# A normalisation cut into steps of one feature tile, which a written order calls between the products at every stage boundary; squares and modulation are deferred

## The chip, the cores and the metric

The kernel runs on one core of one Trainium2 chip. The metric is the device time of one launch in microseconds (us); a number given for a kernel is the median of its runs.

## The reference, cut to what matters

Two layers of a diffusion backbone. Context tokens (128) and latent tokens (512) go through the same weights, with a modulation row of their own each.

```python
mod = einsum('bd,de->be', silu(cond), w_mod) + b_mod
sh1, sc1, g1, sh2, sc2, g2 = split(mod, 6)
h = rms_norm(x, norm1) * (1 + sc1) + sh1
# three branches from h @ w_in: Fourier mixing, gated linear attention, differential attention
merged = gf * y_f + gg * y_g + gd * y_d
x = x + g1 * (merged @ w_out)
h2 = rms_norm(x, norm2) * (1 + sc2) + sh2
ff = (silu(h2 @ w_ff_gate) * (h2 @ w_ff_up)) @ w_ff_down
x = x + g2 * ff
```

`rms_norm` divides a token by the root of the mean of its 1024 squared features. So a layer has two points at which every feature of a token must be there before the next product can start: between `w_out` and the FFN, and between the FFN and the mixer of the next layer. The second layer has no mixer behind it.

## The kernel before, in words

**Tiles.** Activations lie with features on the partitions: 8 tiles (`KT`) of 128 features by 640 tokens. Tokens are worked in two halves of 320, `SPLIT[0]` and `SPLIT[1]`, called p=0 and p=1; p=0 holds the 128 context tokens and 192 latent ones, which have different modulation, so that its instructions often come as a piece of 128 and a piece of 192. Every f32 operand is split into a high part (a cast to a reduced format, on ACT: `wh`, `ah`, `mh`, `h2h`) and a low part (the rest, a subtraction: `wl`, `al`, `ml`, `h2l`), and a product is three matmuls, high-high, high-low and low-high (`acc3`, L471; `advance_to`, L495, for one k step of a product). A product of 320 tokens over 8 feature tiles is 24 matmuls. Weights are loaded by SP into `raw`, cast by ACT (L429) and subtracted by POOL (L433); `used(l, u)` gives a weight's buffers free and starts the split of the weight that is due next. Some FFN weights need sums of blocks first, which DVE makes (L401, L402).

**Order.** PE's order is the order of the code in the whole kernel. In the FFN, DVE, ACT and POOL take their work in the order of the code too (`FFN_ORDERED`); elsewhere a scheduler orders those three. Each engine works in its order, so that an instruction that waits holds up everything behind it on its engine.

**Side work.** `queue(gen)` sets a generator on a side list, of which `slot(cols)` runs one step after each 250 columns of products. `back` is a background generator that `slot` steps after each `rate` columns; `fill` is one that the FFN steps after each group of a down projection that `groups % 4` lets through.

**Stages of a layer.** The mixer ends with the merges (`merge`, L1369 and L1370, on gates `tg`, sums `mg`, products `y`), and w_out follows: 16 products in `NORM_ORDER`, four tiles with both halves, then tiles 4 to 7 of p=0, then those of p=1. After each, `residual` (L1392, DVE) adds it to x, ACT stores x, ACT squares it (L757) and DVE adds the square to `acc` (L758). After the last product of a half, the normalisation `modulate` is queued. Its first step, `norm_diag`, sums `acc` over the partitions with three small matmuls (L766), scales the sums (`ms_v`, L768), takes the reciprocal root in ten small DVE steps (`rs_y`, L613 to L617) and spreads it on a diagonal (`diag`, L771). The second step, `norm_rows`, makes of the diagonal a row for all partitions (L784) and runs through all eight feature tiles: in front of the FFN with `norm_keep` (DVE L797, ACT L799 and L800, low part on DVE or POOL L802), in front of the mixer with `norm_apply` (DVE L847, low part L855 to L859).

**FFN.** `ffn_start` (L1511) makes 4 units of p=0 together, k step by k step, in four half banks of the two `big` PSUM tiles, then 3 units of p=1 in two `main` banks and one `misc` bank. Units are gate and up in turn; `evict` takes them out of PSUM with tanh on ACT, gate (L1559) and up (L1561) on DVE, and a split (L464 ACT, L465 DVE) into the activations `ah`, `al`; `tt` is the tile that they work on. Between them `combine` makes sums of h2 for later Strassen products (`gated`, with its sums `e`, L558). An FFN has four parts, each closed by a down projection into residuals (L1392) and, in the last part, by the squares and the normalisation of the next mixer (`done`).

**Modulation.** `mod_next` makes modulation rows: for each of the 128-feature tiles 16 to 47, per layer, two loads `rawm` and four DVE products (`junk`, L734, 128x512) whose accumulators are added to a mod row (L738). For layer 1, tiles 16 to 39 are made as `fill` in the FFN of layer 0, and tiles 40 to 47 as background work at the start of the mixer of layer 1, at a rate of one step each 320 columns. The first mixer products (`units`, `advance`) use the same four half banks.

## Time and profile before

| | before |
|---|---|
| median of 3 runs | 2406.77 us (2403.03 to 2408.39) |
| the profiled execution | 2402.18 us, of it 2400.4 in the span of the engines |
| PE (matmul), PEld (weight load) | 2244.5 us (94%), 2194.4 us (91%) |
| DVE | 1636.1 us (68%) |
| ACT | 999.8 us (42%) |
| POOL | 964.0 us (40%) |
| DMA | mean 113 GB/s |
| mean granted clock of PE | 0.974 |

The busy time of an engine is the sum of its instructions; the share is that of the span. A granted clock of 1.00 is 2.4 GHz, 0.50 is 1.2 GHz. Layer 0 reaches from 0 to about 1200 us, its FFN from about 740; the FFN of layer 1 begins at about 1940.

### The profile page before, as it was taken

What the parts mean: (1) busy time and instruction counts of PE and PEld (TensorE: products, weight loads), DVE (VectorE), ACT (ScalarE), POOL (GpSimd) and SP (SyncE); (2) the same over time, 40 slices, a digit from 0 to 9 for tenths busy, and PEclk for the clock granted to TensorE, in tenths of its full rate; (3) what the DMA queues carried; (4) which work ended last, traced back from release to release, by engine and by line L of the source; (5) the groups of instructions that cost most, each with busy time, mean ns of one, the idle gap of its engine ahead of it and who ended that gap; (6) DMA issues with size and microseconds to landing.
All of it is one profiled execution on the core that took longest, in us unless ns stands there. A gap on an engine that the chain in (4) does not pass through costs nothing.

```text
span 2400.4 us, 44466 instructions
## 1 busy us (share of the span) xinstructions
PE 2244.5 (94%) x16882; PEld 2194.4 (91%) x16882; DVE 1636.1 (68%) x3398; ACT 999.8 (42%) x2194; POOL 964.0 (40%) x783
## 2 busy tenths in 40 slices
PE   6988999999998899999969999999999988999999
PEld 4888899999997889999968999999999978999999
DVE  5896887676945768778678766876742457475674
ACT  3443546454334424242424545464543344242432
POOL 1344644353324423442433445443523235352533
PEclk9999999999998999999979999999999989999999
DMA  7442221213522272836334322212113221524433
GB/s 266 154 144 85 81 72 54 67 54 104 191 90 86 69 252 84 271 112 211 127 117 141 109 75 72 69 54 67 54 62 115 88 85 56 173 85 162 136 106 123
DMA packets 151381, 271.39 MB, mean 113 GB/s; under 512 B 19200, under 2 KB 31360, under 8 KB 151168
## 3 DMA queue, kind: packets, MB, share of 16 engines
q1 hardware_dynamic: 125824, 219.75, 28.4%
q10 hardware_dynamic: 25344, 48.80, 5.8%
q8 instruction: 133, 2.18, 0.4%
q14 instruction: 80, 0.66, 0.1%
HBM read 235.98 MB, written 27.79 MB: 110 GB/s over the span
## 4 chain that ended last, share of the span: by engine, by line
PE 63%; DVE 18%; issue 6%; ACT 4%; POOL 4%; DMA 3%; ACTq 0%; SPq 0%; POOLq 0%; DVEq 0%
PE main L471 45%; PE misc L471 8%; DVE junk L734 4%; PE big L1279 2%; PE misc L1330 2%; POOL wl L433 1%; DMA x<-xd 1%; POOL ek L1066 1%; DVE w L1211 1%; ACT wh L429 1%; PE big L987 1%; DVE x L1392 1%; DVE tg L1369 1%; PE misc L1310 1%; PE big L495 1%
## 5 line engine op out<-in xcount | busy, mean ns | idle before, releaser
L433 POOL TENSOR_TENSOR wl<-raw,wh 128x512 fp32r<-128x512 f32 x514 | 710.3, 1395 | 1072.9 <-ACT wh L429 857.9
L429 ACT CAST wh<-raw 128x512 fp32r<-128x512 f32 x518 | 316.8, 619 | 275.1 <-PE main L471 187.2
L471 PE MATMUL main<-hh,wh 128*128 128x320 f32 x960 | 302.5, 315 | 2.2 <-DVE aT L1449 2.2
L471 PE MATMUL main<-hh,wl 128*128 128x320 f32 x960 | 297.4, 310 | 0.0
L471 PE MATMUL main<-hl,wh 128*128 128x320 f32 x960 | 297.3, 310 | 0.0
L471 PE MATMUL main<-wh,hh 128*128 128x256 f32 x800 | 234.7, 293 | 7.6 <-ACT tm L604 4.7
L471 PE MATMUL main<-ah,wh 128*128 128x320 f32 x704 | 223.5, 317 | 18.5 <-DVE x L1392 18.4
L471 PE MATMUL main<-wl,hh 128*128 128x256 f32 x800 | 229.1, 286 | 0.0
L471 PE MATMUL main<-wh,hl 128*128 128x256 f32 x800 | 228.9, 286 | 0.0
L734 DVE SCALAR_TENSOR_TENSOR junk<-rawm,cond 128x512 bf16<-128x512 f32 x256 | 217.1, 848 | 14.5 <-DMA rawm<-in_w_modt_dram 10.0
L471 PE MATMUL main<-al,wh 128*128 128x320 f32 x704 | 220.7, 314 | 0.0
L471 PE MATMUL main<-ah,wl 128*128 128x320 f32 x704 | 220.6, 313 | 0.0
L1392 DVE SCALAR_TENSOR_TENSOR x<-main,g,x 128x128 f32<-128x128 f32 (+2 forms) x240 | 96.8, 435 | 163.9 <-PE main L471 151.2
L429 ACT CAST wh<-big 128x512 fp32r<-128x512 f32 x152 | 89.2, 587 | 254.0 <-DVE big L412 75.0
L471 PE MATMUL main<-h2h,wh 128*128 128x320 f32 x536 | 171.0, 319 | 18.1 <-DVE tt L1559 17.6
L471 PEld LDWEIGHTS main<-hh,wh 128*128 128x128 f32 x960 | 181.2, 189 | 2.9 <-DVE aT L1449 2.6
L471 PEld LDWEIGHTS main<-hl,wh 128*128 128x128 f32 x960 | 181.1, 189 | 0.1
L471 PEld LDWEIGHTS main<-hh,wl 128*128 128x128 f32 x960 | 180.8, 188 | 0.0
L471 PE MATMUL main<-h2l,wh 128*128 128x320 f32 x536 | 169.6, 316 | 0.0
L471 PE MATMUL main<-h2h,wl 128*128 128x320 f32 x536 | 169.4, 316 | 0.0
L471 PEld LDWEIGHTS main<-wh,hh 128*128 128x128 f32 x800 | 156.1, 195 | 10.4 <-ACT tm L604 5.3
L471 PEld LDWEIGHTS main<-ah,wh 128*128 128x128 f32 x704 | 135.1, 192 | 23.7 <-DVE x L1392 11.7
(340 smaller groups left out, 6127.1 us busy)
## 6 DMA issues: line engine op xcount, KB each, us to landing
raw<-in_w_dram SPq DMA_DIRECT2D x556, 256.0 KB, 2.9
rawm<-in_w_modt_dram SPq DMA_DIRECT2D x128, 256.0 KB, 4.5
x<-xd ACTq DMA_DIRECT2D x64, 320.0 KB, 4.5
rawm<-in_w_mod_dram SPq DMA_DIRECT2D x64, 256.0 KB, 5.4
xd<-x ACTq DMA_DIRECT2D x48, 320.0 KB, 4.1
xd<-x ACTq DMA_DIRECT2D x48, 160.0 KB, 2.0
cond<-in_cond_b_dram SPq DMA_DIRECT2D x16, 256.0 KB, 4.8
x<-in_x_t_dram SPq DMA_DIRECT2D x12, 320.0 KB, 5.7
```

Source lines behind the costliest of these rows:

```text
L429: nc.scalar.copy(h, raw)
L433: (nc.vector if late or sums else nc.gpsimd).tensor_sub(lo, raw, h.bitcast(F32))
L471: mm = lambda w, x, first=False, last=False: nc.tensor.matmul(ps, w, x, start=first and not more, stop=last, skip_group_check=more)
L495: self.nc.tensor.matmul(ps, a, b, start=(k == 0 and n == 0), stop=(k == KT - 1 and n == 2))
L734: nc.vector.scalar_tensor_tensor(self.sm([P, 512], "junk", 1, mybir.dt.bfloat16), raw, 1.0, cond[i, k], op0=ALU.mult, op1=ALU.mult, accum_ ...
L987: nc.tensor.matmul(ps[64 * x : 64 * x + 64, o : o + 64], kk[r, ks], qq[r, qs], start=True, stop=True)
L1066: nc.gpsimd.tensor_mul(ek, ek, k)
L1211: nc.vector.tensor_mul(hv(wm)[:, :, a, b], hv(x[:, 1:])[:, :, a, 1 - b], hv(sn)[:, :, a, b])
L1279: nc.tensor.matmul(S[:, x], q[:, c : c + P], k, start=(y == 0), stop=(y == 1))
L1310: nc.tensor.transpose(ps[:, o + (x - a) * P : o + (x - a + 1) * P], p[:, x * P : (x + 1) * P], self.c("ident"))
L1330: nc.tensor.matmul(ps, wT[:, x * P : (x + 1) * P], v, start=(x == 0), stop=(x == n - 1))
L1392: nc.vector.scalar_tensor_tensor(x[:, r], ps[:, r.start - s.start : r.stop - s.start], g[:, m, i : i + 1], x[:, r], op0=ALU.mult, op1=ALU.add)
```

## The change

The normalisation becomes a generator that stops behind the diagonal (it yields -3), and then behind each feature tile (`norm_keep` and `norm_apply` yield the index of the last tile whose low part is made). `upto(norm, k)` runs it to tile k in the order of the code on DVE, ACT and POOL. At w_out the steps of p=0 are called between the products of p=1: the diagonal behind product (4,1), then up to tile 0, 2 and 4 behind (5,1), (6,1) and (7,1). In the last down projection of the FFN they are called up to the diagonal, not at all, and up to tile 0 and 1. `first_four` then makes the first four units of the FFN, and of the mixer of layer 1, with the rest of the tiles a k step ahead of their use; the diagonal of p=1 is made behind k=1, its rows and tiles from k=4 on. The square of a tile is taken one product later, and its add two products later. `Gated` takes the first units of the FFN out in another order: gate, gate, up, up, then the low parts, which POOL makes; the eighth product (unit 3 of p=1) goes into a half bank of a `big` tile. The modulation of layer 1 is `fill` for tiles 16 to 31 only, in other groups and not in the last part, and tiles 32 to 47 are made in the mixer of layer 1 from the last gates on, one step each 256 columns.

```diff
+class Gated:
+    def __init__(self, kernel):
+        self.nc, self.tt, self.out = kernel.nc, kernel.unit("tt"), kernel.pairs("a", 1)[0]
+    def gate(self, ps, p):
+        t = self.tt[:, SPLIT[p]]
+        self.nc.scalar.activation(t, ps, AF.Tanh, scale=0.5)
+        self.nc.vector.scalar_tensor_tensor(t, t, 1.0, ps, op0=ALU.add, op1=ALU.mult)
+    def up(self, ps, p):
+        s = SPLIT[p]
+        self.nc.vector.tensor_mul(self.tt[:, s], self.tt[:, s], ps)
+        self.nc.scalar.copy(self.out[0][:, s], self.tt[:, s])
+    def low(self, p):
+        s = SPLIT[p]
+        self.nc.gpsimd.tensor_sub(self.out[1][:, s], self.tt[:, s], self.out[0][:, s].bitcast(F32))
...
+    def first_four(self, l, us, act, norms):
+        self.begin(l, us)
+        first, self.banks = self.banks, None
+        for k in range(KT):
+            self.upto(norms[0], min(k + 1, KT - 1))
+            for i in range(4):
+                self.advance_to(first[i], act, k, i)
+            if k == 1:
+                self.upto(norms[1], -3)
+            elif k >= 4:
+                self.upto(norms[1], k - 5)
+            if k % 2:
+                self.slot(HT)
+        second = [b[:, :HT] for b in (self.main(), self.main(), self.misc())]
+        for k in range(KT):
+            self.upto(norms[1], min(k + 1, KT - 1))
+            for i in range(3):
+                self.advance_to(second[i], act, k, i, 1)
+            if k % 2:
+                self.slot(HT)
+        return first, second
...
+    def squares(self, acc, x, s, m):
+        sq, add = self.square_add(acc, x, s, m == 0)
+        self.after(1, sq)
+        self.after(2, add)
+        if m == KT - 1:
+            self.behind(True)
...
+            yield x - 1
...
     def modulate(self, xs, acc, scale, mod, shift0, p, out, keep=False):
 
-        yield
         dg = self.norm_diag(acc, STARTS[p])
-        yield
+        yield -3
         rb = self.norm_rows(self.misc(), dg[:, : 2 * P], dg[:, 5 * 64 : 6 * 64])
-        with self.tc.manual_schedule(engines={mybir.EngineType.DVE, mybir.EngineType.Activation}):
-            if keep:
-                self.norm_keep(xs, rb, scale, mod, shift0, p, out)
-            else:
-                self.norm_apply(xs, rb, scale, mod, shift0, p, out, range(KT), lambda k: k % 4 == 1)
+        if keep:
+            yield from self.norm_keep(xs, rb, scale, mod, shift0, p, out)
+        else:
+            yield from self.norm_apply(xs, rb, scale, mod, shift0, p, out, range(KT), lambda k: k % 4 == 1)
+    def upto(self, norm, k):
+        with self.tc.manual_schedule(engines=FFN_ORDERED):
+            while norm[1] < k:
+                norm[1] = next(norm[0])
...
-        if len(backs) > 1:
-            self.finish_back()
-            self.back, self.rate = backs[1], 128
+        self.finish_back()
+        self.back, self.rate = backs[1], 128 if l == 0 else 256
...
+        first, second = self.first_four(l, us[:4], h2, norms)
+        acts = [pair(f) for f in range(AHEAD // 2)]
+        for f in range(2):
+            acts[f].gate(first[2 * f], 0)
+        for f in range(2):
+            acts[f].up(first[2 * f + 1], 0)
+        next(combine)
+        for f in range(2):
+            acts[f].low(0)
+        self.used(l, us[0])
+        self.used(l, us[1])
+        acts[0].gate(second[0], 1)
+        acts[1].gate(second[2], 1)
+        acts[0].up(second[1], 1)
+        last = self.big()[:, :HT]
+        self.group_to(last, self.weight(l, us[3]), h2, SPLIT[1])
+        next(combine)
+        acts[0].low(1)
+        acts[1].up(last, 1)
+        self.used(l, us[2])
...
-                if last:
-                    done(xs, m, s)
-                elif p == 0:
+                if not last and p == 0:
                     nc.scalar.dma_start(self.xd[m * P : (m + 1) * P], xs.pop(m))
                     load(m + 2)
                 half.add(m)
-                if fill is not None and groups % 4:
+                if last:
+                    self.behind()
+                    done(xs, m, s)
+                elif fill is not None and groups % 5:
...
+            mg, x2 = self.mixer(l, h, small, (None, later_mod(32, 48)) if l else (later_mod(16, 36), later_mod(36, 48)), norms)
...
+            def norm_steps(m, p, gen, *at):
                 if m == KT - 1:
-                    self.queue(self.modulate(x2, acc, scale2, mod, 24, p, h2, True))
-                self.slot(s.stop - s.start)
+                    norms.append([gen(p), -4])
+                if m > 3 and p and at[m - 4] is not None:
+                    self.upto(norms[0], at[m - 4])
+            with self.tc.manual_schedule(engines=FFN_ORDERED):
+                for m, p in NORM_ORDER:
+                    s = SPLIT[p]
+                    self.residual(x2[m], self.group(self.weight(l, U_OUT + m), 0, KT, mg, s), s, g1, m)
+                    self.behind()
+                    nc.scalar.dma_start(self.xd[m * P : (m + 1) * P, s], x2[m][:, s])
+                    self.squares(acc, x2[m], s, m)
+                    if p == (m > 3):
+                        self.used(l, U_OUT + m)
+                    norm_steps(m, p, lambda p: self.modulate(x2, acc, scale2, mod, 24, p, h2, True), -3, 0, 2, 4)
+                    self.slot(s.stop - s.start)
...
+            def done(xs, m, s):
+                nc.scalar.dma_start(self.xd[m * P : (m + 1) * P, s], xs[m][:, s])
+                self.squares(n_acc, xs[m], s, m)
+                if m == KT - 1 and s.start == 0:
+                    self.finish_back()
+                    keep.append(self.pairs("h", KT))
+                norm_steps(m, int(s.start > 0), lambda p: self.modulate(xs, n_acc, scale1, n_mod, 0, p, keep[0]), -3, None, 0, 1)
...
+                    l, h2, x2, combine, sums, first, g2, done, self.mod_later(l + 1, n_small, n_mod, scale1), self.mod_next(l + 1, 16, 32, n_small, n_mod)
```

**DVE from w_out into the FFN, layer 0.** Below are DVE's rows where the first FFN units leave PSUM: gates and ups of `tt`, low parts `al`, and the sums of raw weights in `big_9391`. First before the change.

```order
L1559 SCALAR_TENSOR_TENSOR tt_9351<-tt_9351,big_9120 128x320
L1561 TENSOR_TENSOR tt_9351<-tt_9351,big_9120 128x320
L465 TENSOR_TENSOR al_9353<-tt_9351,ah_9352 128x320
L1559 SCALAR_TENSOR_TENSOR tt_9359<-tt_9359,big_9121 128x320
L1561 TENSOR_TENSOR tt_9359<-tt_9359,big_9121 128x320
L465 TENSOR_TENSOR al_9361<-tt_9359,ah_9360 128x320
L401 TENSOR_TENSOR big_9391<-raw_9108,raw_9110 128x512
L402 TENSOR_TENSOR big_9391<-raw_9106,raw_9108 128x512
L1559 SCALAR_TENSOR_TENSOR tt_9351<-tt_9351,main_9276 128x320
L1561 TENSOR_TENSOR tt_9351<-tt_9351,main_9277 128x320
L465 TENSOR_TENSOR al_9353<-tt_9351,ah_9352 128x320
L1559 SCALAR_TENSOR_TENSOR tt_9359<-tt_9359,misc_9278 128x320
```

Now with the change; the rows of x (L876 to L880) are a step of `combine`.

```order
L293 SCALAR_TENSOR_TENSOR tt_9423<-tt_9423,big_9119 128x320
L293 SCALAR_TENSOR_TENSOR tt_9426<-tt_9426,big_9120 128x320
L297 TENSOR_TENSOR tt_9423<-tt_9423,big_9119 128x320
L297 TENSOR_TENSOR tt_9426<-tt_9426,big_9120 128x320
L876 TENSOR_TENSOR x_1585_8064<-x_1585_8064 128x320
L878 TENSOR_TENSOR x_1585_8064<-x_1589_8068,x_1585_8064 128x320
L879 TENSOR_TENSOR x_1589_8068<-x_1589_8068,x_1585_8064 128x320
L880 TENSOR_TENSOR x_1589_8068<-x_1589_8068 128x320
L293 SCALAR_TENSOR_TENSOR tt_9423<-tt_9423,main_9307 128x320
L293 SCALAR_TENSOR_TENSOR tt_9426<-tt_9426,misc_9309 128x320
L297 TENSOR_TENSOR tt_9423<-tt_9423,main_9308 128x320
L876 TENSOR_TENSOR x_1586_8065<-x_1586_8065 128x320
```

The four steps on the first banks (`big`) follow each other now, no low part stands among them, and no sum of raw weights stands ahead of the steps on `main` and `misc`; a step of `combine` does instead.

**DVE in the last down projection of the FFN, layer 0.** These rows are the residuals of tiles 4, 5 and 6, p=0, and what stands between them, before the change: an add of a square into `acc` directly behind each residual, products of the modulation (`junk`) and a row of it.

```order
L1392 SCALAR_TENSOR_TENSOR x_2682_14108<-main_14350,g_1650_8434,x_2682_14108 128x128
L1392 SCALAR_TENSOR_TENSOR x_2682_14108<-main_14350,g_1650_8434,x_2682_14108 128x192
L758 TENSOR_TENSOR acc_9117<-acc_9117,sq_14369 128x320
L1392 SCALAR_TENSOR_TENSOR x_2683_14110<-main_14372,g_1650_8434,x_2683_14110 128x128
L1392 SCALAR_TENSOR_TENSOR x_2683_14110<-main_14372,g_1650_8434,x_2683_14110 128x192
L758 TENSOR_TENSOR acc_9117<-acc_9117,sq_14391 128x320
L734 SCALAR_TENSOR_TENSOR junk_14396,modsum_14345<-rawm_14302,cond_10155 128x512
L734 SCALAR_TENSOR_TENSOR junk_14398,modsum_14345<-rawm_14302,cond_10159 128x512
L738 SCALAR_TENSOR_TENSOR mod_227<-modsum_14345,small_225 128x2
L1392 SCALAR_TENSOR_TENSOR x_2684_14112<-main_14401,g_1650_8434,x_2684_14112 128x128
L1392 SCALAR_TENSOR_TENSOR x_2684_14112<-main_14401,g_1650_8434,x_2684_14112 128x192
L758 TENSOR_TENSOR acc_9117<-acc_9117,sq_14420 128x320
```

With the change, from the residual of tile 5 of p=0 on (x_2684 here, since the tile names are given anew).

```order
L1453 SCALAR_TENSOR_TENSOR x_2684_14185<-main_14402,g_1650_8434,x_2684_14185 128x128
L1453 SCALAR_TENSOR_TENSOR x_2684_14185<-main_14402,g_1650_8434,x_2684_14185 128x192
L804 TENSOR_TENSOR acc_9116<-acc_9116,sq_14379 128x320
L1453 SCALAR_TENSOR_TENSOR x_2685_14187<-main_14424,g_1650_8434,x_2685_14187 128x128
L1453 SCALAR_TENSOR_TENSOR x_2685_14187<-main_14424,g_1650_8434,x_2685_14187 128x192
L804 TENSOR_TENSOR acc_9116<-acc_9116,sq_14401 128x320
L1453 SCALAR_TENSOR_TENSOR x_2686_14189<-main_14446,g_1650_8434,x_2686_14189 128x128
L1453 SCALAR_TENSOR_TENSOR x_2686_14189<-main_14446,g_1650_8434,x_2686_14189 128x192
L804 TENSOR_TENSOR acc_9116<-acc_9116,sq_14423 128x320
L804 TENSOR_TENSOR acc_9116<-acc_9116,sq_14445 128x320
L804 TENSOR_TENSOR acc_9116<-acc_9116,sq_14467 128x320
```

The add behind a residual is now that of the square of the tile two products back, the last three adds come together, and no modulation products stand there.

**DVE from the merges into w_out, layer 1.** The last merge (gates `tg`, sums `mg`, low parts `ml`) and the first residuals of w_out (x), before the change.

```order
L1369 SCALAR_TENSOR_TENSOR tg_21856<-tg_21856,y_22287 128x320
L1370 TENSOR_TENSOR mg_17740<-mg_17740,tg_21856 128x320
L465 TENSOR_TENSOR ml_21936<-mg_17740,mh_21935 128x320
L1392 SCALAR_TENSOR_TENSOR x_4124_21937<-main_22329,g_4188_22305,x_4124_21937 128x320
L1392 SCALAR_TENSOR_TENSOR x_4124_21937<-main_22357,g_4188_22305,x_4124_21937 128x128
L1392 SCALAR_TENSOR_TENSOR x_4124_21937<-main_22357,g_4188_22305,x_4124_21937 128x192
L1392 SCALAR_TENSOR_TENSOR x_4125_21938<-main_22398,g_4188_22305,x_4125_21938 128x320
L758 TENSOR_TENSOR acc_22312<-acc_22312,sq_22425 128x320
L1392 SCALAR_TENSOR_TENSOR x_4125_21938<-main_22428,g_4188_22305,x_4125_21938 128x128
L1392 SCALAR_TENSOR_TENSOR x_4125_21938<-main_22428,g_4188_22305,x_4125_21938 128x192
L758 TENSOR_TENSOR acc_22312<-acc_22312,sq_22468 128x320
L1392 SCALAR_TENSOR_TENSOR x_4126_21939<-main_22471,g_4188_22305,x_4126_21939 128x320
```

With the change, at the same place.

```order
L1430 SCALAR_TENSOR_TENSOR tg_21844<-tg_21844,y_22359 128x320
L781 SCALAR_TENSOR_TENSOR junk_22386,modsum_22379<-rawm_22320,cond_21320 128x512
L1431 TENSOR_TENSOR mg_17630<-mg_17630,tg_21844 128x320
L781 SCALAR_TENSOR_TENSOR junk_22388,modsum_22379<-rawm_22320,cond_21324 128x512
L486 TENSOR_TENSOR ml_21945<-mg_17630,mh_21944 128x320
L785 SCALAR_TENSOR_TENSOR mod_227<-modsum_22379,small_225 128x2
L781 SCALAR_TENSOR_TENSOR junk_22394,modsum_22393<-rawm_22377,cond_21318 128x512
L1453 SCALAR_TENSOR_TENSOR x_4060_21946<-main_22469,g_4188_22443,x_4060_21946 128x320
L781 SCALAR_TENSOR_TENSOR junk_22396,modsum_22393<-rawm_22377,cond_21322 128x512
L781 SCALAR_TENSOR_TENSOR junk_22400,modsum_22393<-rawm_22384,cond_21320 128x512
L781 SCALAR_TENSOR_TENSOR junk_22402,modsum_22393<-rawm_22384,cond_21324 128x512
L785 SCALAR_TENSOR_TENSOR mod_227<-modsum_22393,small_225 128x2
```

Products of the modulation now stand between the steps of the merges and between the residuals.

## Rows read from the trace of the kernel before

**Rows 1.** Windows: from:to length, then busy (instructions) of PE, PEld, DVE, ACT, POOL, PEclk, DMA, GB/s

```profile
720.00:816.00 96.00, 76.43 (x446) 73.96 (x446) 60.99 (x118) 42.76 (x93) 41.32 (x33) 0.88 0.21 65
1196.00:1280.00 84.00, 58.13 (x290) 55.33 (x289) 66.88 (x181) 24.85 (x55) 26.85 (x27) 0.78 0.42 140
1918.00:2014.00 96.00, 76.78 (x446) 74.58 (x445) 61.25 (x118) 42.75 (x93) 40.80 (x33) 0.87 0.21 65
1842.00:1876.00 34.00, 30.16 (x192) 28.05 (x192) 27.57 (x48) 17.19 (x40) 10.79 (x8) 1.00 0.34 110
1876.00:1894.00 18.00, 18.00 (x124) 18.00 (x125) 4.64 (x10) 5.52 (x11) 6.31 (x5) 1.00 0.34 106
2060.00:2380.00 320.00, 319.34 (x2172) 318.20 (x2171) 201.78 (x340) 114.82 (x211) 128.78 (x94) 1.00 0.39 129
```

**Rows 2.** Windows of two stretches behind waits, same columns

```profile
728.59:731.80 3.21, 3.21 (x15) 3.21 (x14) 1.66 (x5) 1.25 (x3) 0.00 (x0) 0.50 0.35 123
790.16:793.20 3.04, 3.04 (x11) 3.04 (x12) 2.80 (x4) 0.46 (x1) 1.57 (x2) 0.50 0.00 0
```

**Rows 3.** Waits of PE, 720 to 816: sum in us, count, longest

```profile
PE main L471 <- DVE tt L1559: 8.8, 2, 6.4
PE main L471 <- DVE tt L1561: 3.3, 1, 3.3
PE misc L784 <- DVE diag L771: 2.6, 1, 2.6
PE misc L471 <- DVE e L558: 2.5, 1, 2.5
PE main L495 <- ACT h2h L800: 1.7, 1, 1.7
```

**Rows 4.** Waits of PE, 1190 to 1285

```profile
PE main L471 <- DVE x L1392: 9.1, 3, 5.5
PE big L495 <- POOL wl L433: 4.6, 2, 2.7
PE misc L784 <- DVE mod L738: 3.7, 1, 3.7
PE misc L784 <- DVE diag L771: 3.5, 1, 3.5
PE big L495 <- ACT wh L429: 2.7, 1, 2.7
```

**Rows 5.** Timeline of DVE and POOL at the norm chains: start, duration, then wait in brackets

```profile
721.95 1.16 DVE L613 TENSOR_SCALAR rs_y<-ms_v 128x3 int32<-128x3 int32 x1
721.80 1.29 POOL L433 TENSOR_TENSOR wl<-raw,wh 128x512 fp32r<-128x512 f32 x1 [0.46 <-PE misc L766]
...
1235.00 0.15 DVE L768 TENSOR_SCALAR ms_v<-misc 128x3 f32<-128x3 f32 x1
1237.15 0.56 DVE L771 TENSOR_TENSOR diag<-const,rs_y 128x384 f32<-128x384 f32 x1
```

**Rows 6.** Lines of DVE, 1190 to 1285: count, busy us, mean ns, idle before

```profile
L734 DVE SCALAR_TENSOR_TENSOR junk<-rawm,cond 128x512 bf16<-128x512 f32 x34 | 28.2, 831 | 0.4
L1392 DVE SCALAR_TENSOR_TENSOR x<-main,g,x 128x192 f32<-128x192 f32 (+2 forms) x22 | 8.9, 430 | 0.4 <-PE main L471 0.4
L758 DVE TENSOR_TENSOR acc<-acc,sq 128x320 f32<-128x320 f32 x14 | 7.5, 533 | 18.0 <-ACT sq L757 18.0
```

**Rows 7.** Timeline of DVE in the last FFN part, one add

```profile
1198.37 0.49 DVE L758 TENSOR_TENSOR acc<-acc,sq 128x320 f32<-128x320 f32 x1 [5.82 <-ACT sq L757]
```

**Rows 8.** Lines of DVE (740 to 830) and of POOL (700 to 830)

```profile
L465 DVE TENSOR_TENSOR al<-tt,ah 128x320 fp32r<-128x320 f32 x6 | 5.2, 862 | 3.6 <-ACT ah L464 3.6
L802 POOL TENSOR_TENSOR h2l<-x,h2h 128x320 fp32r<-128x320 f32 x8 | 7.6, 949 | 17.1 <-ACT h2h L800 17.1
```

**Rows 9.** The page, DMA issues: count, KB of each, us from issue to landing

```profile
rawm<-in_w_modt_dram SPq DMA_DIRECT2D x128, 256.0 KB, 4.5
```

**Rows 10.** Waits of ACT, 1842 to 1876: sum, count, longest

```profile
ACT mh L464 <- DVE mg L1370: 15.3, 15, 2.0
```

More of the change, by code (lines that the diff above doesn't have):

```diff
@@ L1417, in rgate, with mixer @@
                 )
-    def mixer(self, l, h, small, backs):
+    def mixer(self, l, h, small, backs, norms):
         nc = self.nc
-        if backs:
-            self.back, self.rate = backs[0], 160 if len(backs) > 1 else 320
+        if backs[0] is not None:
+            self.back, self.rate = backs[0], 160
         tab = {}
@@ L1428, in mixer, with evict @@
         us, fold = [self.unit("u") for _ in range(4)], []
-        for i, ps, s in self.units(l, [U_UF + g for g in range(4)], h, 4):
+        def evict(i, ps, s):
             nc.scalar.copy(us[i][:, s], ps)
@@ L1432, in mixer @@
                 fold.append(self.folds(us[i]))
+        if norms is None:
+            for x in self.units(l, [U_UF + g for g in range(4)], h, 4):
+                evict(*x)
+        else:
+            u = range(U_UF, U_UF + 4)
+            banks = self.first_four(l, u, h, norms)
+            for i, ps in enumerate(banks[0]):
+                evict(i, ps, SPLIT[0])
+            for i, ps in enumerate(banks[1]):
+                evict(i, ps, SPLIT[1])
+                self.used(l, u[i])
+            evict(3, self.group(self.weight(l, u[3]), 0, KT, h, SPLIT[1]), SPLIT[1])
+            self.used(l, u[3])
+            self.slot(HT)
         fact = self.pairs("f", 4)
@@ L1536, in ffn_start, with ffn @@
         for _ in combine:
             pass
-    def ffn(self, l, h2, x2, combine, sums, g2, done, back=None, fill=None):
+        return {f: a.out for f, a in enumerate(acts)}
+    def ffn(self, l, h2, x2, combine, sums, norms, g2, done, back=None, fill=None):
         nc = self.nc
@@ L1545, in ffn @@
             last = fp == len(FF_PARTS) - 1
[L1546 removed]
+            act, xs = {}, {}
             def load(m):
```

127 lines of the change are left out of this document (49 added, 78 removed).

## Prediction

> **What bounds the kernel now.** I read the windows first, then the waits of TensorE (PE) in the three stage boundaries, then the engine that ended each wait. The windows give a yardstick: from 2060 to 2380 us PE never waits, and 2172 matmuls take 320 us, 0.1473 us each at a granted clock of 1.00, the 2.4 GHz level [rows 1]. Any other window can be priced with it. In layer 0, from the last products of w_out into the FFN (720 to 816 us), 446 matmuls would take 65.7 us and take 96: 30.3 lost. The same boundary of layer 1 (1918 to 2014) has 446 matmuls too and loses 30.3. From the last down projection of layer 0 into the mixer of layer 1 (1196 to 1280), 290 matmuls would take 42.7 us and take 84: 41.3 lost [rows 1]. So three boundaries lose 101.9 us.
>
> Each loss has two parts. One is waiting. At the first boundary: 8.8 us and 3.3 us for activations of the first FFN units to leave PSUM (tt), 2.6 for the diagonal of the norm, 1.7 for the first normalised tile, 2.5 for a sum of the first Strassen products [rows 3]; the boundary of layer 1 repeats this. At the mixer: 9.1 us for the residual, 3.7 and 3.5 for the two diagonals (the first is charged to a mod row queued just ahead of it), 7.3 for weights that ACT and POOL split late [rows 4]. The other part is the clock: after a wait of about 2 us and more the granted clock is 0.50, the 1.2 GHz level. In 728.59 to 731.80, behind the wait for the diagonal, 15 matmuls take 3.21 us, where 0.1473 each makes 2.2; from 790.16 on, 11 take 3.04 instead of 1.6 [rows 2]. A wait of 2 us or more thus costs 1.0 to 1.4 us more; I use 1.4.
>
> DVE is what PE waits for, since it takes its work in order. From 1190 to 1285 it spends 28.2 us on 34 modulation products (junk, 831 ns each) and stands 18.0 us at the adds of the squares until ACT has squared [rows 6]. The longest of these: ACT is held by the loads of x, the add stands 5.82 us for its square, and the next residual, hence a PSUM bank, stands behind the add [rows 7].
>
> **The change, boundary w_out to FFN (twice).** Matmul counts stay; PE does the same products, with the norm's few matmuls moved by some k steps. Term by term, for one boundary of 30.3 us:
> - Activations leaving PSUM: before, gate, up, cast and low part of each unit stood in one chain, and two sums of raw weights (L401, L402) ahead of the next gate. Now four steps for the first banks follow each other, the low parts go to POOL, and the eighth product goes to a free bank of `big` instead of a `main` bank. The banks it takes were filled by the first 96 products, and 72 more (10.6 us) lie between. The 12.1 us of tt waits go [rows 3], and with them three clock falls, 4.2.
> - Tiles of p=1: rows are made after k=4 of the first products, not after them, so the wait of 1.7 us for the first tile goes [rows 3], with its fall, 1.4.
> - The diagonal of p=0: its matmul keeps its place, one product after the sums. The ten small steps and the diagonal take 2.7 us where POOL is still (1235.00 to 1237.71) and were stretched where POOL splits weights: a 0.16 us step takes 1.16 until POOL's 1.29 us end [rows 5]. The splits fall in the same products. I take no gain: 2.6 plus a fall of 1.4 stay. Bounds: 0 and 4.
> - New waits. The split of the fourth FFN unit now stands behind the last residual and its store on ACT: a residual of 0.43 [rows 6] and a POOL split of 1.29 [rows 5] in a row, about 1.9 with the store's issue, plus 0.7, since a wait of this size stands at the edge of a fall (bounds 0 and 3.3). DVE takes the chain of p=1 at k=1 ahead of the sixth tile of p=0, which costs about 1.0 at k=6. The sums of weights now stand ahead of `up` of the sixth unit: 0.5. Of the other 6.9 us of this boundary's loss, the 2.5 for the Strassen sum with its fall and small waits behind the same DVE backlog, I leave 0.9.
> Left: 2.6+1.4+1.9+0.7+1.0+0.5+0.9 = 9.0 of 30.3. Gain 21.3, twice 42.6.
>
> Six low parts per boundary move from DVE (862 ns each) to POOL, where such a row takes 949 ns [rows 8]; by these rows alone DVE would win 5.2 us. The Trainium skill (SBUF — State Buffer, section "SBUF: two separate sides") says that DVE instructions with two SBUF inputs and GpSimd instructions share one port pair, held exclusively for a whole instruction. By that, DVE would win nothing, for POOL's 5.7 us hold it up as long. The stretched step of the chain agrees [rows 5]. I book zero; they lie off the path.
>
> **Boundary FFN to mixer.** The last FF part no longer carries modulation products (eight tiles less in FFN and the head of the mixer, none in the last part), so 28.2 us leave DVE there, and the squares are added two products later, so that the 18.0 us of standing go [rows 6]. A product of the last part is 15 matmuls, 2.2 us; DVE then needs one or two residual instructions of 0.43 and an add of 0.53 [rows 6]. The hold of ACT by the loads remains, but an add stands two products further back, 4.4 us against 5.82 [rows 7], and I take the rest as covered by the second bank. That takes the 9.1 us and the wait of both diagonals down. Left by my count: 1.2 for the first rows; 3.0 for the third and fourth weight split, still late behind the squares; 3.8 at k=3, where the low part of tile 3 stands on DVE behind the chain of p=1, which begins only when k=1 is done; 1.6 for PSUM copies that ACT makes behind four weight casts; three falls 4.2. Sum 13.8 of 41.3, gain 27.5. Bounds: all three falls and half the waits gone, 33; every wait doubled, 18.
>
> **Tail of mixer 1 (a cost).** Sixteen tiles of modulation, 64 products, move to the end of the mixer of layer 1. By the order, 30 stand before the merges, where DVE idles; 19 stand between the merges and 15 in the first w_out products. One takes 0.83 us [rows 6] and some 0.08 for its accumulator, 0.91. Between the merges DVE is already busy 27.57 of 34 us [rows 1], and PE hangs on it through ACT, which waits 15.3 us for DVE there [rows 10]. 19 products are 17.3 us; the 6.4 of idle time can take some. Cost 10.9 if it takes all it can, 17.3 if nothing; I take 14, half way, since the idle pieces lie scattered. In the first w_out products DVE is busy 4.64 of 18 us [rows 1] and gets 13.7 more: just even, but unevenly laid, 3 (up to 6). Tail: 17, bounds 9 (the pieces hide better than counted) and 28 (falls of the clock as well).
>
> **Sum.** 42.6 + 27.5 - 17 = 53.1. On the profiled execution of 2402.2 us that gives 2349.1; the median of the runs stands 4.6 above that execution, and so I put the median at 2354.
>
> **Rivals.**
> 1. *The waits only move.* DVE and ACT do the same work at the boundaries of the FFN, in order; if the steps between products delay residuals or leave the tiles late, half of the 70.1 us comes back: 2354 + 35 = 2389. For it: the chain at k=1 and POOL's splits in the same stretch. Against: the 18.0 us of standing and the 28.2 us of modulation are gone from one of the three [rows 6].
> 2. *The tail is free.* The 34 products fill idle pieces and PE has a product in hand: 2354 - 17 = 2337. Against it stands DVE's 27.57 of 34 [rows 1].
> 3. *Slower: loads in the tail are exposed.* The 34 products need 17 loads, issued on SP's queue between raw weight loads that wait for buffers; a load lands 4.5 us after its issue [rows 9]. If each were issued only when DVE stands at it, 17 x 4.5 = 76.5 in place of 17: 2413. It decides from about 4.1 us exposed per load ((17 + 53) / 17). Against: the 34 products around the mixer boundary stood 0.4 us in all [rows 6].
> 4. *No effect*: the engines run into the same banks at the same time, 2407.
>
> **Chances.** Forecast 0.52 (its own range 2340 to 2368), waits move 0.25, tail free 0.15, loads exposed 0.05, no effect 0.03. The predicted time is the forecast's. The range 2326 to 2390 leaves out the fourth and third rival and the best of the second. A run of this kernel tells about 0.2% (4.8 us) from no change: faster 0.92, same 0.03, slower 0.05.
>
> **What would show it.** In the changed profile: the boundary windows at about 75 us for 446 matmuls, and 57 us for 290; no tt waits in the first FFN products; the wait for the first diagonal still there at w_out, gone or near 1 us at the mixer; a wait for a low part at k=3 in the mixer's first products; the merges of layer 1 some 14 us longer than those of layer 0, with PE waiting for ACT's y or mh and those for DVE. I would be wrong if DVE stands at a load in the tail, if the boundaries keep clock falls at each k step, or if the splits of weights set the pace behind POOL's low parts.

## The result and the profile after

The changed kernel takes 2371.64 us (median of 4 runs, 2369.35 to 2375.32); the kernel before, on the same chip, 2405.38. The ratio is 0.9861 with a 95% interval of 0.9843 to 0.9878: 33.7 us faster. The profiled executions stand 26.9 us apart (2402.18 and 2375.32). The page of the changed kernel, its span and its first part:

```profile
span 2373.5 us, 44461 instructions
PE 2236.4 (94%) x16882; PEld 2187.4 (92%) x16882; DVE 1639.4 (69%) x3386; ACT 996.0 (42%) x2194; POOL 976.0 (41%) x795
```

DVE's busy time has not fallen: the change moves its work. I read where the time went by stages, each from the start of its first matmul in the timeline to that of the next, in us. Where the experiments below have the same code as the changed kernel, their profiles show how far a row can be trusted: w_out and the last down projection agree to about 1 us, the merges to 2.5 (40.8 to 43.3), the first units of the mixer to 3 (39.8 to 42.8), the first part of an FFN and the third down projection to some 3.5 (99.4 to 102.9 and 106.8 to 110.4), the rest of mixer 1 to 5.5 (538.5 to 544.0), and all ahead of w_out to 7 (674.6 to 682.0), so that its +3.3 tells nothing.

| stage | before | after | difference |
|---|---|---|---|
| all ahead of w_out, layer 0 | 673.4 | 676.7 | +3.3 |
| w_out, layer 0 / layer 1 | 63.8 / 63.8 | 61.1 / 66.9 | -2.7 / +3.1 |
| first FFN products to the first down projection, layer 0 / 1 | 109.0 / 108.0 | 101.0 / 99.9 | -8.0 / -8.1 |
| first and second down projection with the gates and ups behind each | 236.2 | 233.8 | -2.4 |
| third down projection, last gates and ups | 102.3 | 110.4 | +8.1 |
| last down projection, layer 0 | 61.0 | 37.8 | -23.2 |
| first units of mixer 1 | 49.9 | 42.8 | -7.1 |
| rest of mixer 1 up to the last merges | 542.7 | 544.0 | +1.3 |
| last merges of mixer 1 | 32.6 | 40.9 | +8.3 |

Windows of the changed kernel (columns as in [rows 1]). The first three hold the products of the boundary windows of before; then the last merges and w_out of layer 1, and the third FFN stage of the table.

```profile
723.40:807.80 84.40, 71.23 (x447) 69.31 (x446) 61.16 (x112) 42.39 (x94) 47.35 (x39) 0.94 0.23 74
1901.45:1986.30 84.85, 71.61 (x447) 69.69 (x446) 61.20 (x113) 42.91 (x94) 47.83 (x39) 0.93 0.23 74
1194.30:1247.80 53.50, 47.02 (x291) 45.48 (x290) 38.14 (x100) 20.79 (x48) 22.37 (x25) 0.90 0.35 114
1807.70:1848.50 40.80, 31.61 (x193) 29.65 (x192) 35.98 (x82) 15.61 (x37) 11.45 (x9) 0.96 0.46 158
1848.50:1915.40 66.90, 61.49 (x397) 60.30 (x396) 43.77 (x113) 19.53 (x43) 19.07 (x15) 0.95 0.38 132
1072.60:1183.00 110.40, 101.77 (x663) 99.66 (x663) 87.12 (x179) 35.78 (x66) 40.45 (x29) 0.97 0.44 146
```

At 0.1473 us a matmul the two windows at the FFN lose 18.6 and 19.0 us where they lost 30.3 [rows 1], and the one at the mixer 10.6 where it lost 41.3. The waits (sum, count, longest) of PE in the first FFN window, in the third window and in the merges, and of DVE from 1790 to 1860:

```profile
PE misc L492 <- DVE e L598: 3.2, 1, 3.2
PE main L492 <- DVE tt L297: 3.2, 1, 3.2
PE main L492 <- DVE tt L293: 2.6, 1, 2.6
PE big L518 <- ACT wh L450: 1.8, 1, 1.8
PE misc L838 <- DVE diag L825: 1.4, 1, 1.4
PE big L518 <- POOL wl L454: 1.0, 1, 1.0
...
PE big L518 <- POOL hl L914: 4.5, 2, 2.7
PE big L518 <- DVE hl L911: 1.7, 1, 1.7
...
PE main L492 <- ACT y L1426: 9.2, 6, 3.2
...
DVE junk L781 <- DMA rawm<-in_w_modt_dram: 6.4, 6, 2.3
```

Against [rows 3] the wait for the first normalised tile is gone and that for the diagonal has halved; the tt waits (12.1) are 5.8; the wait for e has grown. Against [rows 4] those for the residual (9.1) and both diagonals are gone. DVE's timeline shows why tt still waits (start, duration):

```profile
765.11 0.49 DVE L878 TENSOR_TENSOR x<-x,x 128x320 f32<-128x320 f32 x1
...
771.63 1.27 DVE L876 TENSOR_TENSOR x<-x 128x320 f32<-128x320 f32 x1
773.00 1.40 DVE L878 TENSOR_TENSOR x<-x,x 128x320 f32<-128x320 f32 x1
774.50 1.40 DVE L879 TENSOR_TENSOR x<-x,x 128x320 f32<-128x320 f32 x1
775.94 1.47 DVE L880 TENSOR_TENSOR x<-x 128x320 f32<-128x320 f32 x1
...
778.74 1.94 DVE L423 TENSOR_TENSOR big<-raw,raw 128x512 f32<-128x512 f32 x1
781.72 0.49 DVE L293 SCALAR_TENSOR_TENSOR tt<-tt,main 128x320 f32<-128x320 f32 x1 [1.05 <-ACT tt L292]
...
771.26 5.80 POOL L454 TENSOR_TENSOR wl<-raw,wh 128x512 fp32r<-128x512 f32 x4
```

A step of `combine` takes DVE about 0.5 us an instruction alone and 1.3 to 1.5 while POOL makes four weight splits. Behind the four stand two weight sums (the second is the row at 778.74), behind the second a cast on ACT, behind the cast the tanh of the fifth unit, and behind that the gate (L293) whose PSUM bank PE has waited for since 779.

### The profile page after: what moved, and what is told of

The parts are those of the page before. It is cut to its first block, busy times and chain, and to the rows that moved or that the text cites. A ratio compares the mean times of both kernels' runs of the same rounds, so it can differ in the third digit from the quotient of the medians.

```text
span 2373.5 us, 44461 instructions
## 1 busy us (share of the span) xinstructions
PE 2236.4 (94%) x16882; PEld 2187.4 (92%) x16882; DVE 1639.4 (69%) x3386; ACT 996.0 (42%) x2194; POOL 976.0 (41%) x795
## 5 line engine op out<-in xcount | busy, mean ns | idle before, releaser
L492 PE MATMUL main<-hh,wh 128*128 128x320 f32 x936 | 294.9, 315 | 0.8 <-DVE aT L1526 0.8
L492 PE MATMUL main<-hh,wl 128*128 128x320 f32 x936 | 289.5, 309 | 0.0
L492 PE MATMUL main<-hl,wh 128*128 128x320 f32 x936 | 289.5, 309 | 0.0
L781 DVE SCALAR_TENSOR_TENSOR junk<-rawm,cond 128x512 bf16<-128x512 f32 x256 | 222.8, 870 | 27.6 <-DMA rawm<-in_w_modt_dram 22.8
L492 PEld LDWEIGHTS main<-hh,wh 128*128 128x128 f32 x936 | 176.4, 188 | 1.6 <-DVE aT L1526 1.0
L492 PE MATMUL main<-h2h,wh 128*128 128x320 f32 x520 | 165.8, 319 | 12.7 <-DVE tt L297 6.3
L492 PEld LDWEIGHTS main<-hh,wl 128*128 128x128 f32 x936 | 176.0, 188 | 0.0
L492 PE MATMUL main<-h2l,wh 128*128 128x320 f32 x520 | 164.6, 317 | 0.0
L492 PE MATMUL main<-h2h,wl 128*128 128x320 f32 x520 | 164.5, 316 | 0.0
L492 PEld LDWEIGHTS main<-wl,hh 128*128 128x128 f32 x800 | 158.2, 198 | 0.0
```

Of the source, the lines that this page charges most:

```text
L492: mm = lambda w, x, first=False, last=False: nc.tensor.matmul(ps, w, x, start=first and not more, stop=last, skip_group_check=more)
L781: nc.vector.scalar_tensor_tensor(self.sm([P, 512], "junk", 1, mybir.dt.bfloat16), raw, 1.0, cond[i, k], op0=ALU.mult, op1=ALU.mult, accum_ ...
```

## The experiments

Each kernel is the changed one with one edit, the last with three. Times are medians; the ratio is to the kernel before, as the 0.9861 of the changed kernel is, since the median of the kernel before lay between 2400 and 2405 us from one comparison to the next. Numbers by stage come from one profile of each kernel.

**Squares not deferred.**

```diff
-        self.after(1, sq)
-        self.after(2, add)
-        if m == KT - 1:
-            self.behind(True)
+        sq()
+        add()
```

> The changed kernel, with each square and its add directly behind the residual again; all else stays. Theory F (deferral carries a good part of the gain between FFN and mixer, since DVE stood 18 us at the adds before): 9 to 15 us slower, 2381 to 2387. Theory G (the modulation products leaving the last FFN part carry it, and the adds would be hidden): under 4 us, below 2376.

2386.41 us, ratio 0.9931 (0.9908 to 0.9953). w_out of layer 0 takes 63.9 us again, as before the change, and that of layer 1 70.9 in place of 66.9; the last down projection takes 44.6 in place of 37.8. Theory F holds: the deferral carries 2.8 to 4.0 us at each w_out and 6.8 of the 23.2 there.

**The steps not called between the last products of w_out.**

```diff
-norm_steps(m, p, lambda p: self.modulate(...), -3, 0, 2, 4)
+norm_steps(m, p, lambda p: self.modulate(...), None, None, None, None)
```

> The changed kernel, without the calls of the normalisation's steps between the last products of w_out: the diagonal and the first tiles of p=0 come at the start of the first FFN units. Theory O (calling them between the products carries a part of the gain): PE waits for the diagonal and the first tiles at both FFNs, 4 to 8 us each with a clock fall, 2379 to 2388. Theory P (the rest of the chain hides as well in the first FFN products): within 4 us, 2368 to 2376.

2381.70 us, ratio 0.9916 (0.9892 to 0.994). w_out up to the first FFN product takes 68.6 and 74.5 us, 7.5 and 7.6 more. PE's longest wait from 735 to 765:

```profile
PE misc L838 <- DVE diag L825: 6.5, 1, 6.5
```

Theory O holds, at the upper end of its price.

**The first FFN units taken out in the old order, low parts on DVE.**

```diff
         for f in range(2):
             acts[f].gate(first[2 * f], 0)
-        for f in range(2):
             acts[f].up(first[2 * f + 1], 0)
+            acts[f].low(0)
         next(combine)
-        for f in range(2):
-            acts[f].low(0)
...
-        self.nc.gpsimd.tensor_sub(self.out[1][:, s], ...)
+        self.nc.vector.tensor_sub(self.out[1][:, s], ...)
```

(The second half likewise: gate, up and low part of the first pair, then the next gate.)

> The changed kernel, with the first four FFN units taken out of PSUM in the old order (gate, up, cast and low part of one unit, then of the next) and the low parts on DVE; the eighth product stays in a big bank. If the step of the prediction holds that the order of these instructions carried the tt waits (12.1 us and their falls, per FFN): 10 to 30 us slower, 2382 to 2400. If the free bank for the eighth product and the waiting of others carried it: within 4 us, 2368 to 2376.

2372.08 us, ratio 0.9871 (0.9849 to 0.9894): no difference from the changed kernel that can be told. The waits for tt are 6.7 us in place of 5.8, that for e 3.7 in place of 3.2. The six low parts of each FFN are back on DVE here, so their move to POOL, too, is worth nothing that can be told.

**The eighth product in a main bank.**

```diff
-        last = self.big()[:, :HT]
+        last = self.main()[:, :HT]
```

> The changed kernel, with the eighth product of the first FFN units in a main bank again, not in a free half of a big one. Theory M (that bank is what took the 6.4 us wait for tt away): PE waits for a main bank before this product, 4 to 8 us more in each FFN, 2379 to 2388. Theory N (the banks are free in time either way): within 4 us, 2368 to 2376.

2374.84 us, ratio 0.9878 (0.9849 to 0.9907). PE waits 1.9 us ahead of this product, where it waited 6.4 in the kernel before, but the waits for tt and e from 755 to 818 sum to 8.6, against 9.0 in the changed kernel. Theory N.

**Weight sums asked for later.**

```diff
         acts[1].up(last, 1)
-        self.used(l, us[2])
...
                 if i == 4:
-                    acts[1].low(1) if p == 0 else self.used(l, us[3])
-                elif p:
+                    if p == 0:
+                        acts[1].low(1)
+                        self.used(l, us[2])
+                elif p == 0:
+                    self.used(l, us[3])
+                else:
```

> The changed kernel, with two calls of used moved in the first FFN units: the split of the weights that need sums is asked for behind the gate of the fifth unit and the up of the sixth unit, not ahead of them. Theory D (what is left at the start of the FFN is DVE at weight sums that stand ahead of the gate and the up that free PSUM banks): the waits of 2.6 and 3.2 us go at both FFNs with a clock fall each, about 17 us in all, 2355. Theory E (DVE is late by the sums of combine, stretched while POOL splits weights): the bank waits shrink by a third at most, under 6 us in all, 2366 or above.

2370.31 us, ratio 0.9858 (0.9835 to 0.9882): theory E's time. PE's waits from 755 to 818:

```profile
PE misc L492 <- DVE e L598: 4.2, 1, 4.2
PE main L492 <- DVE tt L293: 2.6, 1, 2.6
PE main L492 <- ACT e L596: 1.3, 1, 1.3
PE main L492 <- DVE tt L297: 1.1, 1, 1.1
```

They sum to 9.2 us, against 9.0. The wait for up (tt L297) has lost 2 us, and those for e have gained them. In the runs so far, order decides who waits for DVE in this stretch, and hardly how long.

**Four weight splits from POOL to DVE.**

```diff
-        self.used(l, us[0])
-        self.used(l, us[1])
         acts[0].gate(second[0], 1)
         acts[1].gate(second[2], 1)
         acts[0].up(second[1], 1)
+        self.used(l, us[0], vec=True)   # low part on DVE
+        self.used(l, us[1], vec=True)
```

> The changed kernel, with the four low parts of the weights of the fifth and sixth FFN unit made by DVE, not by POOL, and asked for behind the three steps on the next banks. Theory I (DVE and POOL hold each other up there: the four sums of combine take 5.8 us beside the four splits where they take 2.0 alone): these four sums take about 2 us, and the gate behind them comes some 1 us earlier although DVE has 2.7 us of work more; time 0 to 4 us faster, 2368 to 2372. Theory J (DVE has too much work, POOL does not matter): the gate comes 2 to 3 us later, and the time is 4 to 8 us slower in the two FFNs, 2376 to 2380.

2366.68 us, ratio 0.9848 (0.9824 to 0.9873). The same place in the timeline:

```profile
772.08 2.50 DVE L454 TENSOR_TENSOR wl<-raw,wh 128x512 fp32r<-128x512 f32 x4 [1.05 <-ACT wh L450]
774.49 0.49 DVE L876 TENSOR_TENSOR x<-x 128x320 f32<-128x320 f32 x1
775.08 0.49 DVE L878 TENSOR_TENSOR x<-x,x 128x320 f32<-128x320 f32 x1
775.68 1.10 DVE L879 TENSOR_TENSOR x<-x,x 128x320 f32<-128x320 f32 x1
776.81 0.49 DVE L880 TENSOR_TENSOR x<-x 128x320 f32<-128x320 f32 x1
...
775.55 0.88 POOL L881 TENSOR_TENSOR tl<-x,th 128x320 fp32r<-128x320 f32 x1 [3.66 <-ACT th L877]
```

The four sums take 2.8 us in place of 5.8; the one that is still long (1.10) stands beside an instruction of POOL. DVE does 2.5 us of work more and is done at the same time. This is theory I's mechanism; its gain in time cannot be told from none, and PE's waits from 755 to 818 sum to 9.0 us here as in the changed kernel. The Trainium skill (SBUF — State Buffer, section "SBUF: two separate sides") says that whichever of a DVE instruction with two SBUF inputs and a GpSimd instruction starts first holds the port pair that they share to its end. The trace agrees: 1.27 to 1.47 us beside splits of 1.45 each, 0.49 without them.

**Modulation out of the tail, into the mixer.**

```diff
         for pr in range(2):
+            if l and pr:
+                self.back, self.rate = backs[1], 320
...
-        self.finish_back()
-        self.back, self.rate = backs[1], 128 if l == 0 else 256
+        if not l:
+            self.finish_back()
+            self.back, self.rate = backs[1], 128
```

> The changed kernel, with the 16 tiles of modulation of layer 1 begun earlier: from the second input of attention on, one step each 320 columns, in place of the last gates and one step each 256. Theory A (the tail of the mixer is longer because DVE makes modulation products between the merges): where the products are done before the merges, the merges take some 36 us again, and the time falls by about 14 us, to 2358. Theory B (the products cost as much wherever they stand in this mixer, since DVE is behind everywhere, or since their loads are late): no more than 4 us change, 2368 to 2376.

2381.29 us, ratio 0.991 (0.988 to 0.994). The tail is as theory A has it: merges 32.5 us in place of 40.9, w_out 61.1 in place of 66.9, 14.2 us back. But the mixer ahead of the merges takes 567.4 in place of 544.0. PE's longest waits from 1610 to 1700:

```profile
PE main L492 <- ACT y L1426: 6.6, 2, 4.4
PE big L1282 <- DVE kT L1238: 6.3, 1, 6.3
```

Neither theory's time: the run is some 10 us slower than the changed kernel, where theory B allowed 4. B's first reason, that DVE is behind everywhere in this mixer, is the nearer one: attention waits for DVE more dearly than the merges do.

**Short products in the tail.**

```diff
+        cols = 16 if l and m0 == 32 else 512
...
-  ..., "junk", ...), raw, 1.0, cond[i, k], ...
+  ..., "junk", ...)[:, :cols], raw[:, :cols], 1.0, cond[i, k][:, :cols], ...
```

> The changed kernel, with the 64 modulation products at the end of mixer 1 made over 16 of their 512 columns; all loads stay and are waited for, the values of tiles 32 to 47 are left out for the rest. Theory A (DVE's time for the products): the tail is some 14 us shorter, 2358. Theory C (DVE stands at loads that come late, 2.3 and 1.1 us in the trace, and what is queued behind it waits): no more than 4 us, 2368 or above.

2363.70 us, ratio 0.983 (0.9807 to 0.9852): between the two theories. w_out falls to 62.0, but the merges stay at 39.3. From 1790 on:

```profile
PE main L492 <- ACT y L1427: 7.8, 6, 4.3
...
DVE junk L782 <- DMA rawm<-in_w_modt_dram: 13.8, 8, 3.8
```

Without its work DVE stands at the loads instead. So loads alone keep most of the price between the merges; in w_out, where the price falls from 5.8 to 0.9 us, it was the products.

**Loads of x between the merges.**

```diff
         for m in range(KT):
-            nc.sync.dma_start(x2[m], (self.xd if l else self.a["x_t"])[m * P : (m + 1) * P])
+            if not l:
+                nc.sync.dma_start(x2[m], self.a["x_t"][m * P : (m + 1) * P])
         for m in range(KT):
             self.merge(l, U_BR[2] + KT + m // 2, m, dact, tg[m], merged, parts=mg[m])
+            if l:
+                nc.sync.dma_start(x2[m], self.xd[m * P : (m + 1) * P])
```

> The changed kernel, with the eight loads of x in mixer 1 issued one behind each merge, not all ahead of the merges, on the same queue. Theory H (half of what the tail costs is DVE standing at modulation loads that queue behind these eight): the waits of DVE for a load between the merges go, with PE's wait of 2.8 us and the falls behind it, 4 to 7 us faster than the changed kernel, 2365 to 2368. Theory A alone (DVE's time for the products): no more than 2 us.

2369.37 us, ratio 0.9863 (0.9841 to 0.9885), no difference. DVE's longest stand at a load from 1790 on falls from 2.3 to 1.3 us, and the merges take 41.7 all the same: PE's 9.2 us of waits for y are 10.4, the last 2.3 of them at the first product of w_out. DVE still stands 4.6 us at modulation loads from 1790 on, of 6.4, so this run does not show the products alone.

**Twice the rate.** `128 if l == 0 else 256` becomes `128`.

> The changed kernel, with one step of the modulation of layer 1 each 128 columns, not 256, from the last gates on: most of the 64 products then stand between the gates, ahead of the merges, where DVE idles in the trace (11 to 18 of 30 us). Theory A (what costs is that the products stand between the merges): 8 to 14 us faster than the changed kernel, 2358 to 2364. Theory B (DVE and the loads are short wherever the products stand, as the earlier start showed): within 4 us of it or slower, 2368 and above.

2370.82 us, ratio 0.9878 (0.9848 to 0.9908). w_out 61.1, but the merges 49.1, with 16.1 us of waits for y: theory B.

**The modulation about where it was.**

```diff
-                elif fill is not None and groups % 5:
+                if fill is not None and groups % 4:
...
-            if fp == len(FF_PARTS) - 2:
+            if last:
                 for _ in fill or ():
                     pass
...
-self.mod_next(l + 1, 16, 32, n_small, n_mod)
+self.mod_next(l + 1, 16, 40, n_small, n_mod)
...
-(None, later_mod(32, 48)) if l
+(None, later_mod(40, 48)) if l      # from the first units on, rate 320
```

> The changed kernel, with the modulation of layer 1 placed about as before the change: tiles 16 to 39 as fill in all four FFN parts of layer 0 (three groups of four), tiles 40 to 47 from the start of mixer 1 on at one step each 320 columns (behind its first units), none at its end. Squares stay deferred. Theory K (the deferral of the squares carries the gain between FFN and mixer, and the move of the modulation only costs): the tail gives back 14 us and the third FFN part up to 8, the last part and the head of the mixer lose 4 to 12, sum 2358 to 2368. Theory L (the modulation leaving the last part carries the gain there): the last part loses some 20 us, sum 2374 to 2382.

2373.07 us, ratio 0.9884 (0.9861 to 0.9907), the same as the changed kernel. Stage by stage against it: third down projection -8.8, merges -8.3, w_out -5.8; last down projection +8.2, first units of the mixer +11.5. The move of the modulation buys 19.7 us and costs 22.9. Of the 11.5 at the first units, most is one wait, 9.4 us, for a low part of the third tile (PE's waits from 1180 to 1275):

```profile
PE big L518 <- POOL hl L914: 13.8, 3, 9.4
```

The 24 tiles are 56 steps of `fill`, the groups of the four parts let 48 through, and the eight that are left run in a row behind the last part. There their 16 products stand between the steps of the normalisation. Before the change it was the same, one product between every two steps of the second diagonal, which took 8.2 us from `rs_y` on; in the changed kernel the same chain takes 2.5 (1231.54 to 1234.07). From the timeline of the kernel before:

```profile
1261.63 0.17 DVE L613 TENSOR_SCALAR rs_y<-ms_v 128x3 int32<-128x3 int32 x1
1261.75 0.69 DVE L734 SCALAR_TENSOR_TENSOR junk<-rawm,cond 128x512 bf16<-128x512 f32 x1
...
1269.25 0.55 DVE L771 TENSOR_TENSOR diag<-const,rs_y 128x384 f32<-128x384 f32 x1
```

**Three edits together.** Fill 16 to 29 (groups % 4, first three parts), 38 to 47 from mixer 1's first units on at rate 320, 30 to 37 in the tail at rate 128; the four splits on DVE; and

```diff
-                self.last_sums(x2, sums)
+                for k, n_after in enumerate((1, 2, 2, 3)):
+                    self.after(n_after, lambda k=k: self.split(x2[k][:, SPLIT[1]], *sums["T3"][k]))
```

> The changed kernel with three edits that the runs point to. Modulation of layer 1: tiles 16 to 29 as fill in the first three FFN parts, three groups of four, tiles 38 to 47 in mixer 1 from its first units on (each 320 columns), tiles 30 to 37 from the last gates on (each 128 columns), so that few products stand between the merges. The low parts of the weights of the fifth and sixth unit on DVE, as in the run that tried it alone. The split of the last sums of combine spread over the first three Strassen products, not ahead of them. If the stage prices add up: 8 us in the third FFN part, 10 to 14 at the end of mixer 1, 5 in the two FFNs and 2 to 6 at the Strassen products, less up to 5 in mixer 1: 2344 to 2354. If DVE is short everywhere and the products cost the same wherever they stand (as in the two runs that moved them as a whole): 2362 to 2372.

2361.78 us (5 runs), ratio 0.9834 (0.9816 to 0.9852): the fastest of all, 39 us faster than before; its median is 9.9 us under that of the changed kernel, though the two intervals overlap. Third stage 101.5, merges 32.6, w_out 61.1, first FFN part 97.5 and 98.1: the prices came in, 8.9 and 14.1 us of them. Then the rest of mixer 1 took 563.6 us, 19.6 more, and kept most of it. That is the time of the second theory, though single prices came in.

## Why the prediction came out as it did

Direction and range held, the forecast's own narrower range (2340 to 2368) did not; the gain is 33.7 us where 51 were forecast.

**w_out to FFN: the term that failed.** 9.0 us were to be left of 30.3 and 18.6 and 19.0 are (windows of 84.4 and 84.9 us, not 75), so that the gain is 11.7 and 11.3 us, not 21.3. "The 12.1 us of tt waits go" is the step: of the three waits [rows 3] that of 6.4 us goes, and the two of 2.4 and 3.3 are still 2.6 and 3.2. It was argued from the distance between the products that fill the banks and those that need them again, and from the order of gates and ups. Old order and old bank, each alone, cost nothing that can be told. What the distance left out is DVE's whole load there: steps of `combine`, weight sums, last sums, and the weight splits on POOL, which stretch the steps of `combine`. For this speak the runs with another order, another bank and four splits on DVE, in which PE's waits from 755 to 818 stay between 8.6 and 10.4 us; no run took work away from DVE there, so that it is argued and not shown. "I book zero; they lie off the path" was said of the moved low parts, and the run that put them back does not speak against it. The weight splits that stretch `combine` had no term at all. The wait for e, put in the remaining 0.9, is 3.2. With these three waits stay their falls of the clock: in 783 to 786 us, behind the first of them, the granted clock is 0.59. The other rows came near (the diagonal 1.4 against 2.6 with no fall behind it, the fourth unit's weights 1.8 and 1.0 against 1.9 and 0.7 for a fall).

What took the wait of 6.4 us away was not isolated. It stood ahead of the eighth product; with the old bank alone 1.9 of it come back. One row of before speaks for the weight sums, which stood ahead of the second gates and waited for a load:

```profile
771.58 1.37 DVE L402 TENSOR_TENSOR big<-raw,raw 128x512 f32<-128x512 f32 x1 [3.99 <-DMA raw<-in_w_dram]
```

DVE stood 3.99 us at it with the gate behind, and the prediction, which counted the sum, did not count this wait. In the changed kernel the same sum comes at 778.74 and waits for no load. No run put it back.

**FFN to mixer: near in size, in part by luck.** 13.8 us were to be left and 10.6 are; the window that was to show 57 us shows 53.5. Three waits are left (1222.89, 1227.40 and 1235.99 in the timeline). That for the low part of the fourth tile was forecast at 3.8 and is 2.7. Those for the first two tiles are 1.8 and 1.7, where 1.2 was put for the first rows. No wait for a late weight split (3.0) or for PSUM copies (1.6) is left, so errors of both signs cancel. Of the 23.2 us of the last down projection the deferral carries 6.8 and the modulation's absence 8.2, by the runs that undo one each. For the rest no run was made: it may go only when both are away, or by the steps called between the products, whose first diagonal PE now takes up after 30 matmuls and not after 15.

**The tail: right in size, wrong in kind.** 17 us were forecast and 14.2 measured (by the run that emptied it), but 8.4 of them between the merges, where 14 were put, and 5.8 in w_out, where 3 were put: two misses that cancel. (18 products stand between the merges and 20 in w_out, where 19 and 15 were counted.) The sign named for it, merges some 14 us longer than those of layer 0, came out as 3.8 (40.9 and 37.1). The term was DVE's time alone. By the run with short products the loads alone would keep some 7 of the 8 us at the merges; that the products alone would keep as much is not shown. Rival 3 named the loads, at 4.1 us a load; the longest stand is 2.3.

**What had no term.** The third down projection with the gates and ups behind it, +8.1 us (4.5 to 8.1 by the profiles with the same code). The forecast counted the fill by tiles, "eight tiles less". In the stage where it remained, four groups of five now carry two products of the modulation each (0.7 to 1.8 us) in place of three of four, 25 products in place of 23, and the down projection takes 46.3 us in place of 44.2. The other 6.0 us come behind it. The 16 tiles are 40 steps, the groups of the three parts let 38 through, and the code runs the two that are left in a row behind the last product. So DVE makes six products without a pause, and the sums of the first Strassen products stand behind them:

```profile
1118.79 0.68 DVE L781 SCALAR_TENSOR_TENSOR junk<-rawm,cond 128x512 bf16<-128x512 f32 x1
...
1125.05 0.48 DVE L598 TENSOR_TENSOR e<-misc,e 128x320 f32<-128x320 f32 x1
```

PE's wait for it, and the window behind the wait, in which 24 matmuls of 3.5 us take 6.5:

```profile
PE misc L492 <- DVE e L598: 3.0, 1, 3.0
1125.58:1132.11 6.53, 6.53 (x26) 6.53 (x27) 2.78 (x5) 2.29 (x5) 1.28 (x1) 0.53 0.51 161
```

In the two runs with three groups of four (the old place of the modulation, and the three edits together) no step is left at this place, and the stage takes 101.6 and 101.5.

Rival 1, that half of the gain at the boundaries comes back, gives 2389; what came back is 19.6 us of the 42.6 at the FFNs, and none at the mixer.

## What to carry to other kernels

Where one engine is short over a whole stretch, a new order moves the wait to the next instruction that needs it: sum its work in the stretch first, the stretching by other engines included. Background work has a price wherever it goes, and it is read from the stage that takes it: here 64 products cost 14 us in the tail and 23 in attention, and the whole move, 19.7 gained and 22.9 paid, was worth nothing. The deferral and the steps between products, which move no work to another stage, carry most of the gain: undoing them costs 16.8 and 13.2 us by the ratios. Price a filler by its rate in each stage, and look where the steps run that its rate leaves over: two of them behind the third part stand behind 6 of the 8 us lost there, eight behind the last part behind most of 11.

## What the runs showed of the hardware that was not expected

How far POOL slows DVE. While POOL made four splits in 5.80 us, DVE got through four sums (771.63 to 777.41) that take 0.49 us each alone: about one instruction of DVE for one of POOL. The small step of [rows 5], which has one input and takes 0.16 us alone, took 1.16 beside a split of 1.29, so that the price is POOL's time and not that of the DVE instruction. What this costs the kernel is not shown: with the four splits on DVE the four sums take 2.8 us, DVE has 2.5 us of other work for it, and PE waits as long as before.
